# Moving one modulation vector, regrouping a feed-forward and rewriting the last norm of a two-layer diffusion transformer on one core

## The chip, the cores and the metric

The kernel runs on one core of a Trainium2 chip. The metric is device time in microseconds (us) of one execution. The kernel before takes 1594.34 us, the median of 3 runs (1590.8 to 1597.15). The profiled execution, from which all rows below come, took 1595.19 us.

## The reference

Two transformer layers over 512 latent tokens and 256 context tokens, width 1024, all float32. Layer 0 has eight neighbourhood-attention (NA) heads and eight latent-attention (MLA) heads side by side, one output projection and a SwiGLU feed-forward of width 2816. Layer 1 has 16 sliding-window heads and the same kind of feed-forward. The context tokens pass layer 0 too. Cut to what matters here:

```
def rms_norm(x, gain=None):
    y = x * rsqrt(mean(x * x, axis=-1) + EPS)          # optionally times gain
def modulate(x, shift, scale):
    return rms_norm(x) * (1 + scale) + shift
# per layer: six vectors from c (and from c_ctx for the context): shift, scale, gate of attention and of feed-forward
mods = silu(c) @ mod_w[l] + mod_b[l]
x = x + gate_a * (heads(modulate(x, shift_a, scale_a)) @ w_out)
h = modulate(x, shift_f, scale_f)
x = x + gate_f * (silu(h @ w_g) * (h @ w_u)) @ w_down
out = rms_norm(x_latent_after_layer_1, final_norm)
```

Inside the MLA heads the compressed queries and keys are normalised as well, with gains of their own.

## The kernel before, in words

Activations lie transposed: 128 features on the partitions, 768 tokens (512 latent, `LATS`, then 256 context, `CTXS`) along the row, 8 such tiles (KT) for the width. Every dense product keeps float32 precision by splitting both operands in a high and a low part and summing three matmuls, high·high, high·low, low·high; these are the lines L335, L337 and L338. A weight tile is loaded by the SyncE queue (SP) to a staging tile `wr`, cast by ScalarE (ACT) to `wh` and subtracted by VectorE (DVE) or GpSimd (POOL) to `wl`.

The program in order of time:

- up to about 60 us: loads, the first norm (`first_norm`, `norm_spread`), two modulation vectors (`mods_pe`) on TensorE (PE);
- to about 177 us: twelve projections of layer 0 (`projections`). After each of their 96 steps `bg` takes on average DBG = 0.38 steps of a background generator, `all_mods`, which computes the other modulation vectors;
- to about 265 us: the NA heads, two at a time (`na_jobs`). While a pair of heads runs, `step` draws on side jobs that `beside` has put in a list (ORDER, by pair; STEPS says how many heads' steps pass between draws): splitting later operands, `latent_norms`, which calls `gained`, and `mla_prepare`;
- to about 400 us: the MLA heads and the output projection;
- to about 1000 us: feed-forward 0. Its 22 hidden panels are worked off in groups (CHUNKS: first panel, count). After each group the down projection adds to a residual kept in DRAM (`home`). The last group goes through `final0`, which calls `output` with two streams, first the latent tokens, then the context, and collects sums of squares for the next norm (`norm1`) while it does so;
- to the end: layer 1, its feed-forward, and `final1`, which calls `output` with two halves of 256 latent tokens and writes the result.

Scale, shift and gate vectors of six are counted by `comp`: 0 shift, 1 scale, 2 gate of attention; 3, 4, 5 the same of the feed-forward. The scale of feed-forward 0, comp 4, belongs to the ones computed on TensorE: four chunks of eight 32-row matmuls (L209, weights in tiles `ph` and `pl` loaded by SP, 16 loads of 256 KB), a copy of the partial sums, and two selecting matmuls with `pick` (L213) that add the partial sums of the 32-row groups. Here they come from `all_mods`, in the middle of the projections.

A norm's reciprocal root is a column, one value per token, and is needed along the row. `rstd` (L388 to L397) sums squares with matmuls against `ones`, takes the root on ACT, the reciprocal on DVE (L391), multiplies the identity by the column (L392, "diag") and multiplies by `ones` on TensorE (L397), all in plain float32. `first_norm` with `norm_spread` (L802, L812) and `gained` (L988, L992) do the same.

The order on each engine is set by a scheduler that simulates the program while it is built (`schedule_with_timeline_sim`); `behind` and `in_turn` add orderings by hand. Every engine, and every DMA queue, then works in its fixed order. Tile tags are rings: `wr`, `wh` and `wl` have three buffers each, PSUM tags s, t, o and d have 3, 2, 1 and 2 banks.

Of the kernel before, what the change touches and what calls it, by code (L numbers as in the profile page):

```python
# [27 lines left out]
CHUNKS = ((0, 4), (4, 4), (8, 4), (12, 4), (16, 3), (19, 3)), ((0, 3), (3, 3), (6, 4), (10, 4), (14, 4), (18, 4))  # L28
# [26 lines left out]
ORDER = ("2", "n3", "m", "")  # L55
AFTER = "012k5678"
DBG = 0.38
# [14 lines left out]
STEPS = ((2, 3, 4, 4), 5, 3)  # L72
# [26 lines left out]
def hybrid_kernel(ctx: ExitStack, tc, I, out):  # L99
# [92 lines left out]
    def mods_pe(l, comp, get):  # L192
# [4 lines left out]
        for c in range(4):  # L197
            o = get()
            for k in range(KT):
                if k % 2 == 0:  # L200
# [9 lines left out]
            t, d = T("p", [P, NX]), get()  # L210
# [86 lines left out]
    def all_mods():  # L297
        for comp in (2, 4, 3, 5):
            yield from component(0, comp)
        for comp in (1, 0):  # L300
            yield from component(1, comp)
        for comp in (2, 4, 3, 5):
            for m in range(KT):
                yield from mod_tile(1, comp, m, (0,))
# [40 lines left out]
    def PQ():  # L345
        return PS("d")
# [32 lines left out]
    def rstd(acc, nfeat, c, r, get=PQ, tag="p"):  # L379
# [4 lines left out]
        col, diag = T("sm", [P, 6, 2]), B(tag=tag)  # L384
        col = col.rearrange("p a b -> p (a b)")[:, :m]
        for i in range(m):
            for j, a in enumerate(accs):
                marks["sum"] = PE.matmul(d[:, i : i + 1], a[:, i * P : (i + 1) * P], ones[:, :1], start=j == 0,  # L388
                                         stop=j == len(accs) - 1)
        marks["root"] = S.activation(col, d[:, :m], AF.Sqrt, bias=eps, scale=1.0 / nfeat)  # L390
        V.reciprocal(col, col)  # L391
        marks["diag"] = V.tensor_tensor(diag[:, :n].rearrange("p (a b) -> p a b", b=P), ident.unsqueeze(1).to_broadcast([P, m, P]),  # L392
                                        col.unsqueeze(2).to_broadcast([P, m, P]), op=ALU.mult)
        for i in range(0, n, 512):
            w = min(512, n - i)
            d = get() if r is not None else PS("o")
            marks["spread"] = PE.matmul(d[:, :w], ones, diag[:, i : i + w], start=True, stop=True)  # L397
# [28 lines left out]
    class Norm:  # L426
# [5 lines left out]
        def add(self, k, c):  # L432
            if c is self.two:
                self.acc = self.acc if k else [None, None]
                i = k // 4
                self.acc[i] = square_sum(self.acc[i], self.src[k], c, eng=(G, V)[i])
                if k == KT - 2:
                    n = c.stop - c.start
                    V.tensor_tensor(self.acc[1][:, :n], self.acc[1][:, :n], self.acc[0][:, :n], op=ALU.add)
                    self.acc[0] = None  # L440
# [358 lines left out]
    def first_norm(acc, c):  # L799
        n, d = (c.stop - c.start) // P, PM()  # L800
        col, diag = T("sm", [P, 6, 2]).rearrange("p a b -> p (a b)")[:, :n], B(tag="p")
# [928 lines left out]
```

## Time and profile before

| what | value |
| --- | --- |
| time, median of 3 | 1594.34 us (1590.8 to 1597.15) |
| profiled execution | 1595.19 us |
| its span, first to last instruction | 1593.4 us |
| mean granted clock of TensorE | 0.988 |
| busy: PE, DVE, ACT, POOL | 96%, 74%, 50%, 19% |
| data moved by DMA | 214.91 MB |

1.8 us of the profiled execution lie outside its span. A row of a timeline reads: start, duration, engine, line, operation, out<-in by the program's names, shape, count, and in brackets the idle time of the engine before it and what ended that. Matmuls are pipelined, so that their durations overlap; the distance from one start to the next is what one costs. A row of the windows reads: stretch, length, busy time of PE, of the weight loads (PEld), of DVE, ACT and POOL with counts, granted TensorE clock, busy share of the DMA engines, GB/s.

### The profile page before, as it was taken

How to read it: one execution, taken by the hardware profiler on the slowest of the kernel's cores; microseconds unless marked ns; L12 is line 12 of the kernel's file. 1: busy time of each engine (PE TensorE's matmuls, PEld its weight loads, DVE VectorE, ACT ScalarE, POOL GpSimd, SP SyncE). 2: the span in 40 equal slices, each digit the busy share in tenths (PEclk: the TensorE clock that was granted, in tenths of full speed). 3: DMA queues.
4: the chain of work that ended last, by engine and by line, in shares of the span. 5: the costliest groups of instructions: out<-in, count | busy, mean ns of one | idle time of the engine just before them, and what ended most of it. 6: DMA issues, size and time to landing. Idle time of an engine off the chain costs nothing. (4 is left out here: it accounts for less than half of the span.)

```text
span 1593.4 us, 26482 instructions
## 1 busy us (share of the span) xinstructions
PE 1533.9 (96%) x9966; PEld 1371.9 (86%) x9966; DVE 1177.1 (74%) x2348; ACT 797.9 (50%) x1615; POOL 299.3 (19%) x322
## 2 busy tenths in 40 slices
PE   6999999999999999999999998999999999999997
PEld 4787767787899999999989896877889899899997
DVE  4885877576678587796858686878877778678685
ACT  4563676775455243342424243557755545354453
POOL 0144623320011101102021202493012000000002
PEclk9999999999999999999999998999999999999998
DMA  9745332104343555637464756121015133324222
GB/s 309 252 129 178 84 117 59 23 6 159 129 162 127 190 168 167 215 114 289 152 248 158 268 165 248 61 87 60 2 46 168 47 100 126 107 79 133 87 93 80
DMA packets 76544, 214.91 MB, mean 135 GB/s; under 512 B 9952, under 2 KB 17504, under 8 KB 76416
## 3 DMA queue, kind: packets, MB, share of 16 engines
q1 hardware_dynamic: 57568, 141.79, 27.0%
q0 software_dynamic: 15968, 67.24, 12.2%
q10 hardware_dynamic: 2880, 4.20, 0.7%
q8 instruction: 78, 1.28, 0.3%
q14 instruction: 50, 0.41, 0.1%
HBM read 186.97 MB, written 23.07 MB: 132 GB/s over the span
## 5 line engine op out<-in xcount | busy, mean ns | idle before, releaser
L324 ACT CAST wh<-wr 128x1024 fp32r<-128x1024 f32 (+2 forms) x148 | 114.7, 789 | 199.8 <-DMA wr<-in_w_dn_dram 35.4
L325 DVE TENSOR_TENSOR wl<-wr,wh 128x1024 fp32r<-128x1024 f32 (+2 forms) x145 | 134.0, 930 | 81.6 <-ACT wh L324 79.9
L555 ACT ACTIVATE p<-p,sm 128x512 f32<-128x512 f32 (+3 forms) x144 | 105.0, 730 | 30.2 <-DVE sm L559 28.3
L376 POOL TENSOR_TENSOR p<-p,p 128x256 f32<-128x256 f32 (+1 forms) x33 | 32.2, 976 | 465.0 <-PE psd L338 340.5
L1372 PE MATMUL pss<-b,wh 128*128 128x384 f32 (+1 forms) x344 | 107.0, 311 | 0.6 <-ACT b L361 0.6
L1373 PE MATMUL pss<-b,wh 128*128 128x384 f32 (+1 forms) x344 | 107.2, 312 | 0.1
L1374 PE MATMUL pss<-b,wl 128*128 128x384 f32 (+1 forms) x344 | 106.2, 312 | 0.4 <-DVE wl L1360 0.4
L233 DVE CUSTOM_DVE_ANT_0 p<-rope,cond 128x1024 bf16<-128x1024 f32 x64 | 77.2, 1222 | 38.3 <-DMA rope<-in_mod_w_dram 38.3
L337 PE MATMUL psd<-b,wh 128*128 128x512 f32 (+3 forms) x256 | 87.9, 344 | 0.0
L335 PE MATMUL psd<-b,wh 128*128 128x512 f32 (+3 forms) x216 | 78.5, 364 | 0.5 <-ACT wh L324 0.3
L549 PE MATMUL pso<-ph,b 128*64 128x256 f32 (+1 forms) x384 | 77.5, 360 | 0.4 <-DVE ph L494 0.2
L549 PE MATMUL pso<-pl,b 128*64 128x256 f32 (+1 forms) x384 | 76.7, 359 | 0.7 <-DVE pl L494 0.7
L338 PE MATMUL psd<-b,wl 128*128 128x512 f32 (+3 forms) x216 | 76.6, 355 | 0.1
L228 POOL DMA_DIRECT2D rope<-in_mod_w_dram x48 | 25.5, 531 | 239.7 <-DVE mod L233 227.0
L1374 PE MATMUL pst<-b,wl 128*128 128x384 f32 (+1 forms) x224 | 70.1, 313 | 0.0
L1373 PE MATMUL pst<-b,wh 128*128 128x384 f32 (+1 forms) x224 | 69.9, 312 | 0.0
L1372 PE MATMUL pst<-b,wh 128*128 128x384 f32 (+1 forms) x224 | 69.9, 312 | 0.0
L335 PE MATMUL pss<-st,wh 128*128 128x512 f32 (+2 forms) x200 | 68.2, 342 | 1.6 <-ACT st L1173 0.8
L338 PE MATMUL pss<-st,wl 128*128 128x512 f32 (+2 forms) x200 | 68.0, 341 | 0.0
L337 PE MATMUL pss<-b,wh 128*128 128x256 f32 (+3 forms) x211 | 67.9, 322 | 0.1
L749 PE MATMUL pss<-st,st 128*128 128x256 f32 (+3 forms) x194 | 60.3, 333 | 6.2 <-DVE sm L559 5.9
L1372 PEld LDWEIGHTS pss<-b,wh 128*128 128x128 f32 x344 | 65.2, 190 | 1.1 <-ACT b L361 0.9
(666 smaller groups left out, 5412.9 us busy)
## 6 DMA issues: line engine op xcount, KB each, us to landing
wr<-in_w_gu_dram SPq DMA_DIRECT2D x88, 512.0 KB, 4.1
rope<-in_mod_w_dram POOLq DMA_DIRECT2D x48, 512.0 KB, 3.8
wr<-in_w_out_dram SPq DMA_DIRECT2D x32, 512.0 KB, 3.5
wr<-in_w_dn_dram SPq DMA_DIRECT2D x64, 256.0 KB, 3.0
p<-home POOLq DMA_DIRECT2D x40, 384.0 KB, 5.4
home<-p POOLq DMA_DIRECT2D x40, 384.0 KB, 4.9
wr<-in_w_in_dram SPq DMA_DIRECT2D x21, 512.0 KB, 4.1
nb<-in_nb_dram SPq DMA_DIRECT2D x16, 384.0 KB, 3.1
```

What stands on the lines that cost most here:

```text
L233: V.tensor_tensor_reduce(out=T("p", [P, D], mybir.dt.bfloat16), in0=w, in1=cond[:, v, :], op0=ALU.mult, op1=ALU.add, scale=1.0, scalar=0.0 ...
L324: behind(S.copy(h, r), *after[:1])
L325: behind((G if eng else V).tensor_tensor(lo, r, f(h), op=ALU.subtract), *after[1:])
L335: ins = PE.matmul(o, wh[:, k], mh[:, c], start=first and k == 0, stop=False)
L337: PE.matmul(o, wh[:, k], ml[:, c], start=False, stop=False)
L338: PE.matmul(o, wl[:, k], mh[:, c], start=False, stop=last and k == n - 1)
L549: ins = PE.matmul(o[64 * i : 64 * i + 64, c], v(kt), t, start=n == 0, stop=n == len(moving[i]) - 1)
L555: S.activation(p[:, c], p[:, c], AF.Exp, bias=nm, scale=-1.0, accum_out=dn)
L749: PE.matmul(o, x, ks[0][:, keys], start=True, stop=False)
L1372: PE.matmul(o, wh, xh, start=first and k == 0, stop=False, skip_group_check=not first)
L1373: PE.matmul(o, wh, xl, start=False, stop=False, skip_group_check=not first)
L1374: PE.matmul(o, wl, xh, start=False, stop=k == 3, skip_group_check=not first)
```

## The change

It has six parts.

1. Scale of feed-forward 0. comp 4 leaves `all_mods`. A new side job "s" (`scales`) runs it beside the first pair of NA heads. Its weights are now loaded by POOL's queue, as two 128x512 loads into each of a `wh` and a `wl` buffer per chunk, and the partial sums are copied to a `wr` buffer. DBG goes from 0.38 to 0.335 and the first entry of STEPS from (2, 3) to (6, 4).
2. Groups of feed-forward 0. The last two of (16, 3) and (19, 3) become (16, 4) and (20, 2). The down weights of the last group, now 2 panels, come by `keep_groups` in three loads (768, 768 and 512 columns) that are issued before the body of the last panel pair; before, eight loads of 384 columns came one for each output row (`kept_w`).
3. Spread of reciprocal roots. In `rstd`, `first_norm` with `norm_spread` and `gained` the diag multiply and the float32 matmul with `ones` go; `spread`, a TensorE transpose of the column broadcast to 128x128, comes in, one for each 128 tokens. In `gained` (by the new `gain`) DVE reads the spread values from PSUM; the ACT copies to SBUF go.
4. `Norm.add` keeps four partial sums (rows 0 to 3, 4 and 5, 6, 7) instead of two that are added at the end; the summing matmuls become 16 for the 512 latent tokens.
5. Parking the residual of layer 1 in DRAM: eight stores move from the ACT queue to the SP queue.
6. `final1` is written out: its own four partial sums per half, the square-root table of ACT asked for right after the last silu, the outputs of the first half two at a time between the matmuls of the second half's rows 5 to 7 and after them, their stores all on SP, the last eight outputs alternating between SP and ACT as before.

```
-CHUNKS = (... (12, 4), (16, 3), (19, 3)), ...
+CHUNKS = (... (12, 4), (16, 4), (20, 2)), ...
-ORDER = ("2", "n3", "m", "")
-DBG = 0.38
-STEPS = ((2, 3, 4, 4), 5, 3)
+ORDER = ("2s", "n3", "m", "")
+DBG = 0.335
+STEPS = ((6, 4, 4, 4), 5, 3)
...
-    def mods_pe(l, comp, get):
+    def mods_pe(l, comp, get, wide=None):
...
+                if k % 4 == 0 and wide:
+                    ws = T(wide[k // 4], [P, 1024])
+                    for i in range(2):
+                        G.dma_start(ws[:, 512 * i : 512 * i + 512], I["mod_wp"][PE_MODS.index((l, comp)), c, k // 2 + i])
...
-            t, d = T("p", [P, NX]), get()
+            t, d = T("wr" if wide else "p", [P, NX]), get()
...
-        for comp in (2, 4, 3, 5):
+        for comp in (2, 3, 5):
             yield from component(0, comp)
...
+    def scales():
+        yield from mods_pe(0, 4, PQ, ("wh", "wl"))
...
-        V.reciprocal(col, col)
-        marks["diag"] = V.tensor_tensor(diag[:, :n].rearrange("p (a b) -> p a b", b=P), ident.unsqueeze(1).to_broadcast([P, m, P]),
-                                        col.unsqueeze(2).to_broadcast([P, m, P]), op=ALU.mult)
+        marks["diag"] = V.reciprocal(col, col)
...
-            marks["spread"] = PE.matmul(d[:, :w], ones, diag[:, i : i + w], start=True, stop=True)
+            for j in range(0, w, P):
+                at = (i + j) // P
+                marks["spread"] = spread(d[:, j : j + P], col[:, at : at + 1].to_broadcast([P, P]))
...
+    def gain(tiles, g0, col):
+        for c in (LATS, CTXS):
+            d, n = PQ(), c.stop - c.start
+            for i in range(n // P):
+                at = c.start // P + i
+                spread(d[:, i * P : (i + 1) * P], col[:, at : at + 1].to_broadcast([P, P]))
+            for j, t in enumerate(tiles):
+                V.scalar_tensor_tensor(t[:, c], t[:, c], gains[:, g0 + j : g0 + j + 1], d[:, :n], op0=ALU.mult, op1=ALU.mult)
+        return tiles
...
+    def keep_groups(k0, kc):
+        n = NT // (kc * P)
+        for a in range(0, KT, n):
+            z = min(a + n, KT)
+            r, t = T("wr", [P, n * kc * P]), [T("nb", [P, NT], F32R) if a == 0 else B(F32R, "st") for _ in range(2)]
...
+                    if l == 0 and j == NFF - 1:
+                        keep_groups(k0, kc)
                     p.body()
...
-        behind(S.dma_start(t, H[k][:, LATS]), norm1.marks[0]["root"])
+        behind(nc.sync.dma_start(t, H[k][:, LATS]), norm1.marks[0]["root"])
...
     def final1(src, hs):
-        keep = lambda src, m: ahead.get(m) or load_w(src(m), len(hs), P, None, "b")
-        output(src, hs, 1, 5, STREAMS1, Norm(H, finished, G if EF else None), (0, 0), None, keep, wait=1)
+        behind(S.activation(T("part", [P, 1]), eps, AF.Sqrt), marks["silu"])
...
+        for c in HALVES:
+            sq, turn = [], []
+            for m in range(KT):
...
+                elif m == 2:
+                    last, col, ins = root(first, PQ())
+                elif m == 3:
+                    d, last = factors(col)
+                elif m > 4:
+                    turn += outputs(d, HALVES[0], (2 * m - 10, 2 * m - 9), (nc.sync,))
...
+                turn.append(add_residual(m, o, 1, 5, 0, c))
+                turn += square(m, c, sq)
...
+        in_turn(turn[-1], ins, *outputs(d, c, range(KT), (nc.sync, S)))
```

In the changed kernel the lines from the scale chunks on lie 6 to 50 further down: L215 and L219 are L209 and L213 of before, L751 and L752 the score matmuls L749 and L750, L1372 the casts L1359.

PE, in the middle of the projections (`pss_1194` is the accumulator of a projection, `ph` and `pl` hold the scale's weights), before:

```order
L338 MATMUL pss_1194<-b_100,wl_1157 128x256
L209 MATMUL psd_1203<-ph_1204,cond_col_63 32x256 x2
L209 MATMUL psd_1203<-pl_1208,cond_col_63 32x256 x2
L209 MATMUL psd_1203<-ph_1212,cond_col_63 32x256 x2
L209 MATMUL psd_1203<-pl_1216,cond_col_63 32x256 x2
L335 MATMUL pss_1194<-b_102,wh_1156 128x256
```

PE, among the score matmuls of the first pair of NA heads, now:

```order
L752 MATMUL pss_1962<-st_657,st_653 128x256
L215 MATMUL psd_1819<-wh_1820,cond_col_63 32x256 x2
L751 MATMUL pss_1983<-st_656,st_653 128x512
L752 MATMUL pss_1983<-st_657,st_653 128x512
L215 MATMUL psd_1819<-wh_1820,cond_col_63 32x256 x2
L215 MATMUL psd_1819<-wl_1827,cond_col_63 32x256 x4
L219 MATMUL psd_1835<-pick_64,wr_1834 128x2 x2
L215 MATMUL psd_1841<-wh_1842,cond_col_63 32x256 x4
```

The chunks have left the rows of dense matmuls and stand in front of score matmuls. Their loads stand on POOL between the last background products (L278), the copies of values for the NA heads (L1139) and the splitting of their keys (L718), now:

```order
L278 TENSOR_TENSOR pl_1686<-pl_1686,cond_66 128x512
L718 TENSOR_TENSOR b_1746<-p_1389,b_1746 64x768
L203 DMA wh_1820<-in_mod_wp_dram 128x512 x2
L203 DMA wl_1827<-in_mod_wp_dram 128x512 x2
L203 DMA wh_1842<-in_mod_wp_dram 128x512 x2
L203 DMA wl_1849<-in_mod_wp_dram 128x512 x2
L718 TENSOR_TENSOR st_2117<-p_1549,st_2117 64x768
```

The third and fourth chunk's loads can only be issued once POOL has finished the L718 above them.

ACT, at the boundary from the last panel pair of feed-forward 0 to `final0` (casts `st<-wr` are those of the last group's down weights, casts `b<-p` and `st<-p` those of hidden panels, `wh` casts belong to the first weights of layer 1), before:

```order
L1359 CAST st_9877<-wr_9876 128x384
L1359 CAST st_9901<-wr_9900 128x384
L324 CAST wh_9896<-wr_9894 128x1024
L1427 ACTIVATE p_9617<-pst_9619 128x384
L1359 CAST st_9920<-wr_9919 128x384
L1359 CAST st_9940<-wr_9939 128x384
L1359 CAST b_9583<-p_9617 128x384 x2
L373 ACTIVATE p_9805<-b_9770 128x512
```

and now:

```order
L1372 CAST st_9728<-wr_9727 128x768
L1372 CAST st_9507<-p_9541 128x384
L1372 CAST st_9734<-wr_9733 128x512
L330 CAST wh_9899<-wr_9897 128x1024
L1435 COPY p_9659<-pss_9660 128x384
L330 CAST wh_9915<-wr_9913 128x1024
L1440 ACTIVATE p_9658<-pss_9660 128x384
L1372 CAST st_9624<-p_9658 128x384 x2
L379 ACTIVATE p_9856<-b_9824 128x512
```

No cast of a down weight stands between the last panel's activation (L1427, now L1440) and its own casts any more.

DVE, at the end (`b_…<-ps…` is the last residual, `p<-b,final_norm,pso` an output), before:

```order
L1223 SCALAR_TENSOR_TENSOR b_12147<-pss_16881,mod_1881_9427,b_12147 128x256
L1612 SCALAR_TENSOR_TENSOR p_16878<-b_12141,final_norm_12838,pso_16779 128x256
L1612 SCALAR_TENSOR_TENSOR p_16898<-b_12143,final_norm_12838,pso_16779 128x256
L1612 SCALAR_TENSOR_TENSOR p_16901<-b_12145,final_norm_12838,pso_16779 128x256
L1612 SCALAR_TENSOR_TENSOR p_16904<-b_12147,final_norm_12838,pso_16779 128x256
L376 TENSOR_TENSOR p_16752<-p_16752,p_16895 128x256
L391 RECIPROCAL sm_16908<-sm_16908 128x2
L392 TENSOR_TENSOR p_16909<-ident_r_86,sm_16908 128x256
```

and now:

```order
L1227 SCALAR_TENSOR_TENSOR b_12127<-pss_16864,mod_1817_9172,b_12127 128x256
L1658 SCALAR_TENSOR_TENSOR p_16880<-b_12125,final_norm_12816,pso_16777 128x256
L1658 SCALAR_TENSOR_TENSOR p_16883<-b_12127,final_norm_12816,pso_16777 128x256
L1648 RECIPROCAL sm_16895<-sm_16895 128x2
L1658 SCALAR_TENSOR_TENSOR p_16901<-b_12113,final_norm_12816,pso_16898 128x256
```

Behind the last residual two outputs of the first half are left instead of four, and the sum (L376) and the diag (L392) are gone.

121 lines of the change are left out of this document (75 added, 46 removed).

## The prediction

> **What bounds the kernel now.** I read the page's engine table and its slices first, then the table of waits, then windows of the stages that the change touches, and last PE's rows at the edges of each.
>
> ```profile
> span 1593.4 us, 26482 instructions
> PE 1533.9 (96%) x9966; PEld 1371.9 (86%) x9966; DVE 1177.1 (74%) x2348; ACT 797.9 (50%) x1615; POOL 299.3 (19%) x322
> PE   6999999999999999999999998999999999999997
> PEclk9999999999999999999999998999999999999998
> ```
>
> PE is busy for 96% of the span, and lacks work in three places: the first slice, the 25th (956 to 996 us) and the last. The granted clock falls in the last two as well. An edit gains by taking time from PE's own row, or by closing those three places; DVE, ACT and POOL matter only where PE waits for them.
>
> ```profile
> 120.00:140.00 20.00, 20.00 (x137) 13.26 (x136) 6.01 (x17) 5.60 (x12) 2.98 (x2) 1.00 0.81 289
> 180.00:200.00 20.00, 17.74 (x140) 14.41 (x140) 16.77 (x45) 16.51 (x44) 13.00 (x8) 1.00 0.47 129
> 200.00:240.00 40.00, 36.14 (x243) 27.75 (x244) 28.76 (x67) 31.41 (x72) 10.78 (x9) 0.91 0.35 113
> 960.00:1000.00 40.00, 33.02 (x168) 27.95 (x168) 25.48 (x43) 15.12 (x28) 12.09 (x16) 0.87 0.67 248
> 1560.00:1594.00 34.00, 22.84 (x177) 21.77 (x176) 18.81 (x44) 9.94 (x22) 8.91 (x12) 0.84 0.20 68
> ```
>
> These windows price the stages. In the projections (120 to 140) PE has no gap: whatever leaves this row is won in full. Beside the first neighbourhood heads PE is idle for 2.3 of 20 us, then for 3.9 of 40: work put there is partly free. The boundary at 960 to 1000 leaves PE idle for 7.0 us at a clock of 0.87, and the last 34 us leave 11.2.
>
> **The change part by part.** *Scale chunks leaving the projections.* On PE each of the four chunks lies between a last L338 of a dense row and the next L335:
>
> ```profile
> 116.80 0.28 PE L338 MATMUL pss<-b,wl 128*128 128x256 f32 x1
> 118.01 0.39 PE L335 MATMUL pss<-b,wh 128*128 128x256 f32 x1
> ...
> 120.14 0.28 PE L338 MATMUL pss<-b,wl 128*128 128x256 f32 x1
> 122.03 0.50 PE L335 MATMUL psd<-b,wh 128*128 128x512 f32 x1
> ...
> 124.66 0.39 PE L338 MATMUL psd<-b,wl 128*128 128x512 f32 x1
> 127.63 0.50 PE L335 MATMUL psd<-b,wh 128*128 128x512 f32 x1
> ...
> 131.44 0.28 PE L338 MATMUL psd<-b,wl 128*128 128x256 f32 x1
> 131.56 0.50 PE L213 MATMUL pss<-pick,p 128*128 128x2 f32 x4
> 132.99 0.39 PE L335 MATMUL psd<-b,wh 128*128 128x256 f32 x1
> ```
>
> A 256-wide dense matmul costs 0.12 (131.44 to the next start at 131.56), a 512-wide one twice that, so the pieces cost 118.01 − 116.80 − 0.12 = 1.09, then 1.77, 2.73 and 1.43: 7.0 us, all of it saved there. The same matmuls come back beside the heads, about 1.0 for the eight of a chunk (the first gap holds just these) and 0.5 for the selecting ones, 6 us in all. The floor of what is paid is 0 (idle time of 2.3 + 3.9 = 6.2 us up to 240 us covers them), the ceiling without a stall 7.0. That idle time is waits for softmax, which do not vanish for being filled:
>
> ```profile
> PE pss L749 <- DVE sm L559: 7.7, 9, 1.8
> ```
>
> Nine waits of 0.9 us each: a chunk of 1.5 us fills one and overhangs by 0.6, and only if the scheduler put it at one. I take half, 3.5 paid, so −3.5 net (−7 to 0). The ACT copies and DVE adds move with the chunks; both engines had the same ones before, and DVE has 3.2 of 20 us free in the window at 180.
>
> What could stop PE is the loads. They change queue, from SP to POOL:
>
> ```profile
> ph<-in_mod_wp_dram SPq DMA_DIRECT2D x16, 256.0 KB, 5.1
> rope<-in_mod_wp_dram POOLq DMA_DIRECT2D x8, 256.0 KB, 3.9
> ```
>
> A load of this size from POOL's queue lands 3.9 us after issue, no slower than from SP. But POOL works in order, and the last two chunks' loads stand behind its own work, of which the longest piece near is
>
> ```profile
> 179.53 2.41 POOL L716 TENSOR_TENSOR b<-p,b 64x768 fp32r<-64x768 f32 x1
> ```
>
> In the trace POOL ends its second L716 at about 185 us, when PE is at the same score matmuls behind which the third chunk now stands; both move about 7 us earlier together. PE may wait up to a landing there, and I leave this inside the 3.5.
>
> *Spread of the latent norms (`gained`).* A float32 matmul against `ones` makes way for transposes:
>
> ```profile
> L992 PE MATMUL psd<-b,ones 128*128 128x512 f32 x4 | 3.2, 886 | 1.2 <-DVE b L988 1.2
> 262.15 0.66 PE L503 MATMUL psd<-ident_r,p 128*128 128x128 f32 x4 [0.19 <-ACT b L468]
> ```
>
> The four L992 entries carry 3.2 us of PE and 1.2 of waiting; each row holds the 512-wide and the 256-wide pair of one group. Four transposes take 0.66, so the twelve take 2.0. PE saves 3.2 + 1.2 − 2.0 = 2.4 at most, nothing if its neighbours then wait for the same DVE results; DVE also loses a diag for each group, so I take −2 (−2.4 to 0).
>
> *Boundary of feed-forward 0.* The number of groups stays six, so residual traffic and the sum of matmuls are unchanged. What changes is what the last panel pair waits for:
>
> ```profile
> 972.13 0.58 PE L335 MATMUL psd<-st,st 128*128 128x512 f32 x1 [2.49 <-DVE p L1429]
> 976.77 0.80 PE L335 MATMUL pst<-b,nb 128*128 128x512 f32 x1 [1.94 <-ACT b L1359]
> 990.19 1.05 PE L388 MATMUL pss<-ones,p 128*128 128x1 f32 x8 [2.56 <-DVE p L376]
> ...
> 974.06 0.51 ACT L1359 CAST st<-wr 128x384 fp32r<-128x384 f32 x1 [3.94 <-DMA wr<-in_w_dn_dram]
> ...
> 970.00:975.00 5.00, 2.71 (x6) 1.62 (x6) 2.38 (x6) 1.05 (x3) 0.38 (x1) 0.73 1.02 402
> 975.00:980.00 5.00, 3.23 (x8) 2.56 (x9) 1.74 (x5) 0.51 (x1) 0.00 (x0) 0.50 1.02 404
> ```
>
> ACT waits 3.94 us for a down-weight load (974.06) before it may cast the hidden panel that stands behind it, and DMA is saturated, share 1.02, while the clock halves. The new order has no such cast there and takes the down weights earlier, in three loads. The three waits are worth 2.5 + 1.9 + 2.6 = 7.0. The clock adds the missing part of it, (1 − 0.73) × 2.71 + (1 − 0.50) × 3.23 = 2.3 us of PE's busy time in those ten. So 9.3 at most from these ten microseconds and the norm; four partial sums shorten the 2.56 in front of the norm's sums (one add of DVE less, against 8 more small matmuls: 1.05 for 8, so +1.0). Against it, the context stream, under which that norm hides, loses a panel: 8 rows × 3 matmuls × 0.12 = 2.9 us of cover. I take −7 (−11 to −2): the first two waits and the clock nearly in full (6.7), the norm's wait by a little.
>
> *End.* The last rows before:
>
> ```profile
> 1580.33 0.28 PE L338 MATMUL pss<-st,b 128*128 128x256 f32 x1
> 1581.80 1.70 DVE L1612 SCALAR_TENSOR_TENSOR p<-b,final_norm,pso 128x256 f32<-128x256 f32 x4 [0.29 <-DMA out_dram<-p]
> 1583.42 0.42 DVE L376 TENSOR_TENSOR p<-p,p 128x256 f32<-128x256 f32 x1
> 1583.89 1.01 PE L388 MATMUL psd<-ones,p 128*128 128x1 f32 x4 [3.28 <-DVE p L376]
> 1585.43 0.42 DVE L392 TENSOR_TENSOR p<-ident_r,sm 128x256 f32<-128x256 f32 x1
> 1585.91 1.22 PE L397 MATMUL pso<-p,ones 128*128 128x256 f32 x2 [1.01 <-DVE p L392]
> 1587.17 3.22 DVE L1612 SCALAR_TENSOR_TENSOR p<-b,final_norm,pso 128x256 f32<-128x256 f32 x8 [1.31 <-PE pso L397]
> ```
>
> Between the last product and the sums lie four outputs of the first half (1.70) and an add (0.42) on DVE; both leave that chain, as the sum of row 7 needs its square alone. The diag (0.42) goes, and the spread falls from 1.22 to two transposes, 0.3 by the row above: −0.9. The sums grow from 4 to 8 matmuls, of which six can run before the last square: taken as 0. Together 1.70 + 0.42 + 0.42 + 0.9: −3.4. The eight outputs (3.22) and the stores stay. Bounds: −5 if the table request and the earlier first half also close part of the other gaps of the last 34 us, −2 if the two outputs still behind the last residual come in front of the reciprocal and cost 0.8 each way.
>
> *Start and the remaining norms.*
>
> ```profile
> PE pst L802 <- DVE p L376: 12.6, 1, 12.6
> 16.28 2.08 PE L812 MATMUL pst<-p,ones 128*128 128x512 f32 x2
> ```
>
> The first wait is for loads and squares, which stay. L812's 2.08 becomes six transposes, 1.0, with the diag in front gone, but the first projections wait for weights too: −1 (−1.5 to 0). The parking stores go from ACT to SP, where DMA issues cost PE nothing: 0; if SP holds a weight load of layer 1 behind them, eight of about 4 us would be visible as PE waits, which the other gaps there do not suggest.
>
> Sum: −3.5 − 2 − 7 − 3.4 − 1 = −16.9. The profiled execution took 1595.19, so 1578.3; the median is 0.85 below the profiled one. I forecast **1578**.
>
> **A page that speaks against it.** The Trainium skill, "TensorE: Matmul & The Clock Gate", section "Part 4: PE-mode transpose", says that transposes do not count as busy time for the clock. The trace speaks against a price here: the clock was 1.00 in a stage full of them.
>
> ```profile
> 280.00:320.00 40.00, 40.00 (x313) 32.50 (x310) 23.88 (x74) 28.58 (x66) 13.11 (x9) 1.00 0.09 20
> ```
>
> **The rivals.** *Loads stop the heads (slower).* If each chunk's loads are issued only after the POOL work in front of them and PE reaches the chunk when that work begins, PE waits 2.4 (L716) + 3.9 (landing) = 6.3 us a chunk, 25.2 for four, and the heads absorb nothing. Then 1595.2 − 7.0 + 7.0 + 25.2 − 13.4 = 1607. It is slower than before from 13.4 / 4 = 3.4 us per chunk; with two chunks, 12.6, it is 1594, no change. For it: the loads stand behind L718 in POOL's order. Against it: only two chunks do, and POOL's idle time lies before them. The Trainium skill, "SBUF — State Buffer", section "SBUF: two separate sides", adds a way to it: a load issued from GpSimd waits for its descriptors while VectorE runs certain operations; the 3.9 us of POOL's loads against 5.1 of SP's do not show it. Chance 0.04.
>
> *The heads absorb nothing and the boundary half.* Scale 0, boundary −3.5, the others −1, −2 and −0.5: −7.0, 1588. For it: DMA was saturated at the boundary, and the same bytes still have to come; earlier loads may only shift the full stretch under the pair before. Chance 0.17.
>
> *The shorter context stream turns the norm into a wait.* The first layer-1 products need `norm1`; with 2.9 us less cover its chain, 1.05 of sums growing to 2.1, ends 4 us later against PE: boundary −3, total −13, 1582. Chance 0.17.
>
> *Transposes cool the clock.* If the clock fell to one half for the norm's 2 to 5 us at four places, some 2 us each go: −9, 1586. Chance 0.05.
>
> *More than the sum.* All upper bounds of scale, boundary and end: −7 − 2 − 11 − 5 − 1 = −26, 1569. For it: the clock at the boundary stays full for longer than the ten microseconds counted, and 11.2 us idle lie in the last window. Chance 0.16.
>
> *Nothing happens:* the scheduler's new order elsewhere in the heads eats the gain, 1594. Chance 0.05.
>
> **How the numbers follow.** The forecast has 0.36, with its own range 1574 to 1582. The cases of 1588 and 1569 belong in the range with their own spread of 2, and I let it end at 1567 and 1590; 1594, 1605 and the tails stay outside, about 0.15. A measurement of this kernel can tell about 0.5%, 8 us, from no change: faster than 1586.4 are the forecast, the norm's wait, the big gain and about half of the 0.22 that lies at 1586 to 1588, 0.80; within it the rest of these and the case of nothing, 0.16; slower 0.04.
>
> **What would show it.** Between 115 and 135 us L338 is followed by L335 without a gap, and the projections end 7 us earlier. Between 170 and 200 PE shows no wait of more than 2 us for a load into `wh` or `wl`; four of 5 us or more would make the slower rival true. At the boundary no ACT cast waits for `w_dn`, the three PE gaps of 1.9 to 2.6 shrink below 1, and the clock stays over 0.9; a new wait of 3 us or more in front of the sums or of layer 1's first products would be the norm's rival. From the last product to the last instruction it is 9.5 us instead of 13. If the projections end earlier but the neighbourhood heads end at the old time, the term of the scale chunks was wrong.

## The result, and the profile after

The changed kernel takes 1605.26 us, the median of 5 runs (1601.7 to 1607.25); the kernel before took 1594.34 (1590.8 to 1597.51). The ratio is 1.0061, with a 95% interval of 1.0041 to 1.0081: slower by 0.4 to 0.8%, where 1578 was forecast. The page of the profiled execution, in the rows that were shown of before:

```profile
span 1605.4 us, 26540 instructions
PE 1543.9 (96%) x10024; PEld 1383.4 (86%) x10024; DVE 1168.4 (73%) x2331; ACT 797.2 (50%) x1607; POOL 303.9 (19%) x332
PE   6999889999999999999999999999999999999998
PEclk9999789999999999999999999999999999999999
```

The gap in the 25th slice is closed, as forecast, and the last slice is a little fuller (8 tenths busy instead of 7). Instead, PE is less busy and its clock falls in slices 5 and 6 (161 to 241 us), where the neighbourhood heads run. The windows:

```profile
100.00:110.00 10.00, 8.21 (x38) 6.65 (x37) 9.78 (x21) 5.73 (x15) 7.42 (x5) 0.83 0.40 116
180.00:200.00 20.00, 14.14 (x77) 8.58 (x77) 11.11 (x25) 10.29 (x25) 15.26 (x14) 0.61 0.74 224
200.00:240.00 40.00, 32.68 (x229) 26.53 (x230) 25.74 (x59) 24.63 (x57) 8.99 (x7) 0.88 0.25 73
960.00:1000.00 40.00, 38.26 (x203) 34.76 (x202) 30.54 (x50) 17.41 (x31) 8.00 (x12) 1.00 0.78 275
1000.00:1005.00 5.00, 5.00 (x38) 4.85 (x38) 2.03 (x3) 1.78 (x2) 0.70 (x1) 0.85 0.34 129
1005.00:1010.00 5.00, 5.00 (x25) 5.00 (x25) 2.00 (x5) 1.71 (x5) 2.19 (x3) 0.50 0.17 39
1560.00:1606.00 46.00, 38.32 (x321) 37.93 (x319) 25.59 (x56) 17.25 (x38) 4.59 (x6) 0.94 0.25 75
```

From 180 to 200 us PE is idle for 5.9 us instead of 2.3 and runs at a clock of 0.61; up to 240 another 7.3 us are idle, where it was 3.9.

To see where time was lost and won I put both timelines of PE side by side and took the time at which the same product stands: the first score matmul of the neighbourhood heads, the first of the MLA heads, the first pair product of feed-forward 0, its 1135th (inside the fourth group), the first product of layer 1, the last pair product of feed-forward 1, and the end of the span. Each number is that time minus the time in the profile of before; what a stage costs is the difference of two neighbours.

| profile of | heads | MLA | FF0 | FF0, group 4 | layer 1 | FF1 last | span |
| --- | --- | --- | --- | --- | --- | --- | --- |
| the change | -3.4 | +10.5 | +9.3 | +16.5 | +12.2 | +14.3 | +12.0 |
| e1, without part 1 | -0.4 | -9.2 | -10.3 | -7.2 | -6.6 | -4.3 | -5.7 |
| e2, part 1 alone | -3.3 | +10.6 | +10.6 | +12.7 | +9.9 | +14.2 | +14.2 |
| e3, quarter loads | -3.8 | -2.0 | -1.8 | +6.1 | +0.8 | +2.5 | +0.5 |
| e4, loads on SP | -5.5 | -2.9 | -7.0 | -4.0 | -7.3 | -5.0 | -7.3 |
| e12, last two on SP | -3.6 | -3.1 | -7.2 | -4.8 | -7.9 | -6.6 | -9.0 |
| e5, part 3 alone | -1.8 | -12.1 | -13.6 | -10.9 | -11.0 | -9.6 | -11.6 |
| e13, part 3 with copies | -1.4 | -11.3 | -12.9 | -10.2 | -12.7 | -11.4 | -13.1 |
| e6, part 2 alone | +1.3 | -3.8 | -4.1 | -3.9 | -5.2 | -1.9 | -2.1 |
| e7, part 6 alone | +2.1 | +0.2 | -0.3 | -1.0 | -0.3 | +0.2 | -1.6 |
| e8, without parts 1 and 2 | -1.7 | -7.7 | -8.6 | -6.6 | -4.8 | -4.5 | -6.7 |
| e9, part 4 alone | -0.7 | -3.6 | -3.8 | -3.5 | -3.5 | -3.2 | -3.6 |
| e11, e4 with DBG 0.295 | -4.7 | -3.2 | -1.0 | +1.3 | -2.1 | -0.8 | -2.6 |

By this table the change won 3.4 us up to the heads, lost 13.9 in the heads, won 1.2 up to feed-forward 0, lost 7.2 in its groups, won 4.3 at the boundary to layer 1, lost 2.1 in layer 1 and won 2.3 at the end: 12.0 us lost. One profile is one execution, and how much that matters can be read from e6, e7 and e9: up to 398 us their four compute engines run the same instructions in the same order as before, and yet their heads take 5.1, 1.9 and 2.9 us less than in the profile of before. So differences of less than about 5 us in the heads mean little, and 13.9 does. For the time of a kernel the medians count: the profile of e1 lies 4.8 us above its own median, that of e5 4.5 below.

What stands in the heads: POOL's rows, then PE's waits of over 1 us (the first row is from the projections).

```profile
179.97 1.82 POOL L718 TENSOR_TENSOR b<-p,b 64x768 fp32r<-64x768 f32 x1
181.73 1.12 POOL L203 DMA_DIRECT2D wh<-in_mod_wp_dram  x2
182.84 1.06 POOL L203 DMA_DIRECT2D wl<-in_mod_wp_dram  x2
183.90 1.06 POOL L203 DMA_DIRECT2D wh<-in_mod_wp_dram  x2
184.95 1.07 POOL L203 DMA_DIRECT2D wl<-in_mod_wp_dram  x2
```

```profile
104.44 0.50 PE L344 MATMUL pss<-b,wl 128*128 128x512 f32 x1 [1.79 <-DVE wl L331]
...
183.90 0.47 PE L751 MATMUL pss<-st,st 128*128 128x512 f32 x1 [1.66 <-DVE sm L561]
195.87 0.58 PE L751 MATMUL pss<-st,st 128*128 128x256 f32 x1 [3.23 <-DVE sm L561]
229.07 0.69 PE L551 MATMUL pso<-pl,b 128*64 128x256 f32 x1 [2.19 <-ACT pl L497]
239.14 0.53 PE L751 MATMUL pss<-b,b 128*128 128x192 f32 x1 [2.87 <-DVE sm L561]
```

The loads of the third and fourth chunk, 2 MB, leave POOL between 181.7 and 186.0, straight behind the second L718. In the same microseconds the heads need a bias tile (`nb`), which SP asks for at 185.65. It usually lands 3.1 us after its issue; in this profile one took 9.3, and DVE stood for it:

```profile
DMA to landing us min/median/max: 2.9/3.1/9.3
```

```profile
195.11 0.69 DVE L561 CUSTOM_DVE_ANT_0 p<-pss,nb 128x512 f32<-128x512 f32 x1 [2.13 <-DMA nb<-in_nb_dram]
```

Before, the slowest landing of a bias tile in these 80 us was 3.3 us by the same view. The scale loads land late in the same burst: their view (L203) has a median of 4.3 us and a longest landing of 9.2. PE's list of waits from 176 to 262 us shows for whom it waited, longest first:

```profile
PE pss L751 <- DVE sm L561: 8.6, 4, 3.2
PE pso L551 <- ACT pl L497: 2.2, 1, 2.2
PE psd L219 <- ACT wr L217: 1.4, 3, 0.5
```

No row of that list is a load into `wh` or `wl`. PE stands for the softmax sums on DVE, and these stand once for a bias tile, once behind PE's own chunks: in PE's order the third chunk lies in pieces around a score matmul that DVE waits for.

```profile
186.07 1.07 PE L215 MATMUL psd<-wh,cond_col 128*32 128x256 f32 x4
187.07 0.80 PE L751 MATMUL pss<-st,st 128*128 128x512 f32 x1
188.22 0.64 PE L215 MATMUL psd<-wh,cond_col 128*32 128x256 f32 x2
191.55 1.08 PE L215 MATMUL psd<-wh,cond_col 128*32 128x256 f32 x8
```

### The profile page after: what moved, and what is told of

Read it like the earlier page. It is cut to its first block, busy times and chain, and to the rows that moved or that the text cites. A ratio compares the mean times of both kernels' runs of the same rounds, so it can differ in the third digit from the quotient of the medians.

```text
span 1605.4 us, 26540 instructions
## 1 busy us (share of the span) xinstructions
PE 1543.9 (96%) x10024; PEld 1383.4 (86%) x10024; DVE 1168.4 (73%) x2331; ACT 797.2 (50%) x1607; POOL 303.9 (19%) x332
## 3 DMA queue, kind: packets, MB, share of 16 engines
q0 software_dynamic: 17248, 71.43, 12.9%
## 5 line engine op out<-in xcount | busy, mean ns | idle before, releaser
L330 ACT CAST wh<-wr 128x1024 fp32r<-128x1024 f32 (+2 forms) x148 | 115.5, 795 | 210.8 <-PE pss L343 38.3
L343 PE MATMUL psd<-b,wh 128*128 128x256 f32 (+2 forms) x258 | 86.8, 337 | 2.0 <-DVE b L1373 1.8
L1387 PE MATMUL pss<-b,wl 128*128 128x256 f32 (+1 forms) x258 | 79.7, 309 | 2.3 <-DVE wl L1373 2.2
L551 PE MATMUL pso<-pl,b 128*64 128x256 f32 (+1 forms) x384 | 78.9, 365 | 2.9 <-ACT pl L497 2.2
L343 PE MATMUL pss<-b,wh 128*128 128x256 f32 (+3 forms) x242 | 79.8, 331 | 0.0
L1385 PE MATMUL pss<-b,wh 128*128 128x256 f32 (+1 forms) x258 | 79.5, 308 | 0.0
L1386 PE MATMUL pss<-b,wh 128*128 128x256 f32 (+1 forms) x258 | 79.3, 307 | 0.0
L551 PE MATMUL pso<-ph,b 128*64 128x256 f32 (+1 forms) x384 | 79.0, 364 | 0.3 <-DVE ph L496 0.2
L341 PE MATMUL pss<-st,wh 128*128 128x256 f32 (+2 forms) x231 | 78.5, 340 | 0.4 <-ACT wh L330 0.4
L344 PE MATMUL pss<-st,wl 128*128 128x512 f32 (+2 forms) x231 | 78.0, 338 | 0.0
L341 PE MATMUL psd<-b,wh 128*128 128x512 f32 (+2 forms) x218 | 76.6, 351 | 0.7 <-DVE st L738 0.7
L344 PE MATMUL psd<-b,wl 128*128 128x512 f32 (+2 forms) x218 | 75.6, 347 | 0.7 <-DVE wl L331 0.6
L1385 PE MATMUL pst<-b,wh 128*128 128x384 f32 (+1 forms) x234 | 72.3, 309 | 0.5 <-ACT b L367 0.5
L1386 PE MATMUL pst<-b,wh 128*128 128x384 f32 (+1 forms) x234 | 72.3, 309 | 0.0
L751 PE MATMUL pss<-st,st 128*128 128x256 f32 (+3 forms) x194 | 61.5, 339 | 7.8 <-DVE sm L561 7.7
L1387 PE MATMUL psd<-b,wl 128*128 128x384 f32 (+1 forms) x210 | 65.2, 313 | 2.7 <-DVE wl L1373 2.7
```

Source lines behind the costliest of these rows:

```text
L330: behind(S.copy(h, r), *after[:1])
L341: ins = PE.matmul(o, wh[:, k], mh[:, c], start=first and k == 0, stop=False)
L343: PE.matmul(o, wh[:, k], ml[:, c], start=False, stop=False)
L344: PE.matmul(o, wl[:, k], mh[:, c], start=False, stop=last and k == n - 1)
L551: ins = PE.matmul(o[64 * i : 64 * i + 64, c], v(kt), t, start=n == 0, stop=n == len(moving[i]) - 1)
L751: PE.matmul(o, x, ks[0][:, keys], start=True, stop=False)
```

## The experiments

All are edits of one of the two kernels; "part" counts as in the list of the change. Each was timed in rounds beside the kernel before; the ratio is to that, and its median in the same group of runs is given where the group changes. The scheduler builds every edit anew, so that an edit can move instructions that it does not name; where the traces show that, the text says so.

**e1: part 1 undone.**

```
-ORDER = ("2s", "n3", "m", "")
+ORDER = ("2", "n3", "m", "")
-DBG = 0.335
+DBG = 0.38
-STEPS = ((6, 4, 4, 4), 5, 3)
+STEPS = ((2, 3, 4, 4), 5, 3)
-        for comp in (2, 3, 5):
+        for comp in (2, 4, 3, 5):
```

> The changed kernel with part 1 undone: the scale chunks go back into the projections, the five other parts stay. Theory A (the scale loads fill the DMA engines while the heads wait for their bias tiles, the stall halves the clock, and this outweighs the rest): the projections end about 3 us later than in the changed kernel, the heads come out 10 to 14 us earlier, and the time is 1590 to 1596. Theory B (the loads are late only because they stand behind POOL's work): the same, 1590 to 1596. Theory C (the scheduler's new order, not the loads, costs the time all over the kernel): no more than 4 us of change, 1601 or more.

Measured 1584.66 us against 1595.19 of before, ratio 0.9950 (0.9935 to 0.9965). With the other five parts in place, moving the scale chunks costs 20.6 us (1605.26 against 1584.66), more than A and B expected, and turns a gain into a loss. Theory C falls. The heads come out 19.7 us earlier than in the change (-9.2 against +10.5).

**e2: the kernel before with part 1 alone.**

```
+ORDER, DBG, STEPS, all_mods, mods_pe and scales as in the change; nothing else
```

> The kernel before with part 1 alone. Theories A and B: slower than before by 8 to 14 us, 1602 to 1608, with the loss between 183 and 240 us. Theory C: within 4 us of before.

1610.97 us, ratio 1.0112 (1.0089 to 1.0135), in A's and B's direction and a little beyond. The heads lose 13.9 us, as in the change. Theory C falls here too.

**e3: a quarter of the bytes.** Each load brings 128 of 512 columns and all matmuls of a chunk use them; the scale of feed-forward 0 is then not the reference's.

```
-                    ws = T(wide[k // 4], [P, 1024])
+                    ws = T(wide[k // 4], [P, 512])
-                        G.dma_start(ws[:, 512 * i : 512 * i + 512], I["mod_wp"][..., c, k // 2 + i])
+                        G.dma_start(ws[:, 128 * i : 128 * i + 128], I["mod_wp"][..., c, k // 2][:, 128 * i : 128 * i + 128])
```

> The changed kernel with a quarter of the bytes in the scale loads: each chunk's two loads per buffer bring 128 columns instead of 512, and all eight matmuls use these (so the scale of feed-forward 0 is not the reference's). Number of loads, queue, order and matmuls stay. Theory A: the bias loads land in about 3 us again, PE's wait near 190 us goes, and the time falls by 6 to 12 us, to 1593 to 1599. Theory B: the loads are as late as before, so no more than 3 us. Theory C: no more than 4 us.

1595.49 us, ratio 1.0003 (0.9984 to 1.0022): 10 us won, as A expected. The loads stand at the same place behind POOL's work. They land in 2.2 us, bias tiles in 4.0 at most, and the heads lose 1.8 us instead of 13.9. From 176 to about 208 us the order on POOL and DVE is that of the change, and that on PE and ACT too, but for four chunk matmuls and one copy; there the bytes alone bring the first product with the values (L551) from 204.3 to 200.2 us. Behind that the order differs, so that the larger half of the gain in the heads is not the bytes' alone.

```profile
wh<-in_mod_wp_dram POOLq DMA_DIRECT2D x8, 64.0 KB, 2.2
wl<-in_mod_wp_dram POOLq DMA_DIRECT2D x8, 64.0 KB, 2.2
```

**e4: all scale loads on SP.**

```
-                        G.dma_start(ws[:, 512 * i : 512 * i + 512], ...
+                        nc.sync.dma_start(ws[:, 512 * i : 512 * i + 512], ...
```

> The changed kernel with the scale loads issued by SP instead of POOL. Theory B: the third and fourth chunk's loads no longer wait behind POOL's work, the stall near 190 us goes, 1593 to 1598. Theory A: the same bytes still meet the bias loads, on whose queue they now stand, so 1601 to 1609. Theory C: within 4 us of the changed kernel.

1587.19 us, ratio 0.9948 (0.9933 to 0.9964): 18 us won with the same bytes, in B's direction and beyond its 1593 to 1598; A did not expect it. Bytes alone are not the cause. PE's order is another one here, though: all of the third and fourth chunk stands in front of the 512-wide score matmul that it lay around in the change.

**e12: only the third and fourth chunk's loads on SP.** The edit names nothing but the queue. The expectation takes PE's order around the chunks to be that of the change; the trace shows that it is not.

```
+                        (G if c < 2 else nc.sync).dma_start(ws[:, 512 * i : 512 * i + 512], ...
```

> The changed kernel with only the third and fourth chunk's loads on SP; the first two stay on POOL. PE's order around them is that of the changed kernel. Theory B (the loads behind POOL's L718 are late and arrive in one burst on top of the bias load): these two carry the loss, so 1586 to 1591. Rival (any load on POOL's queue costs the heads, by POOL's issue time or otherwise): half of the gain of moving all four, 1594 to 1599.

1587.22 us against 1593.17, ratio 0.9964 (0.9945 to 0.9983), inside B's range: the loss against the kernel before hangs on the queue of these two chunks' loads. SP's and PE's timelines, and the windows to be set beside those of the change:

```profile
179.62 0.81 SPq L203 DMA_DIRECT2D wh<-in_mod_wp_dram  x2
180.59 0.80 SPq L203 DMA_DIRECT2D wl<-in_mod_wp_dram  x2
```

```profile
181.91 0.64 PE L215 MATMUL psd<-wh,cond_col 128*32 128x256 f32 x8
184.46 0.64 PE L215 MATMUL psd<-wh,cond_col 128*32 128x256 f32 x8
187.89 0.50 PE L751 MATMUL pss<-st,st 128*128 128x512 f32 x1 [1.94 <-DVE sm L561]
```

```profile
180.00:200.00 20.00, 16.25 (x143) 13.22 (x142) 12.93 (x39) 14.20 (x37) 10.04 (x6) 1.00 0.56 178
200.00:240.00 40.00, 36.58 (x281) 28.16 (x280) 32.48 (x75) 31.16 (x74) 11.98 (x9) 1.00 0.38 118
```

The last loads leave at 181.4 instead of 186.0, the chunks run at 181.9 and 184.5 instead of 186 to 197, and the clock is 1.00 in these windows. With the queue the order has changed on PE, DVE and ACT: the chunks now fill the place where PE stood idle in the change (182.2 to 183.9), in front of the score matmul instead of around it, and DVE's splitting of keys (L732, 4.75 us in one piece in the change) comes behind the softmax. A first reading of mine, that the bias tile is the price, is too simple: in e12 DVE waits 6.1 us in all for bias tiles, in the change 6.5, and yet PE keeps its clock. A and B each hold part of it: loads behind POOL's L718 leave late (B) and come in one burst with the bias load (A); less of the burst (e3) or another queue (e4, e12) takes away most of the loss. No run moves the loads with the order of the engines held, so that lateness and the order that the scheduler makes of it are not told apart.

**e5: the kernel before with part 3 alone**, the spreads by transposes in `rstd`, `first_norm`, `norm_spread` and `gained`, as in the diff of the change.

> The kernel before with part 3 alone (the spreads by transposes in the start, the norms and the latent norms). The scale-less run left the neighbourhood heads 8.8 us earlier against before, though this part was priced at -2 there. Theory A (the spread through DVE and float32 matmuls stalled PE and with it cost clock near 210 and 245 us, so that its removal is worth several times its own duration): the heads end 6 to 9 us earlier and the time is 1585 to 1590. Theory B (the 8.8 us come from another part's effect on the order): 1590 to 1594, the heads 0 to 3 us earlier.

1588.10 us against 1592.18, ratio 0.9959 (0.9942 to 0.9975): 4 us won. In its profile the heads win 10.3 us, more than A's 6 to 9, but against the heads of e6, e7 and e9, which are those of before, it is 5.2 to 8.4. Two windows of e5 answer the two cold places of before:

```profile
210.00:220.00 10.00, 9.65 (x73) 7.83 (x72) 8.82 (x21) 9.21 (x23) 5.21 (x6) 1.00 0.24 68
240.00:250.00 10.00, 9.83 (x78) 8.23 (x77) 8.46 (x18) 7.46 (x18) 1.41 (x2) 1.00 0.32 92
```

The same windows of the kernel before:

```profile
210.00:220.00 10.00, 8.70 (x35) 5.57 (x34) 5.25 (x13) 6.72 (x16) 2.35 (x1) 0.66 0.22 68
240.00:250.00 10.00, 7.38 (x47) 6.72 (x43) 7.31 (x12) 3.23 (x11) 4.64 (x4) 0.76 0.00 1
```

Only the first of the two belongs to the program: from 208 to 220 us e6, e7 and e9 have clocks of 0.72 to 0.78 as before has (0.72), but from 240 to 250 all three have 1.00.

**e13: e5 with the copies of the spread values to SBUF kept**, so that only the diag and the float32 matmuls go.

```
+            S.copy(r[:, c], d[:, :n])
+        for j, t in enumerate(tiles):
+            V.scalar_tensor_tensor(t, t, gains[:, g0 + j : g0 + j + 1], r, op0=ALU.mult, op1=ALU.mult)
```

> The kernel before with part 3 alone (1588.1), but with ACT's copies of the spread values to SBUF kept in the latent norms, so that only the diag on DVE and the float32 matmuls go. Theory A (the float32 matmul chain behind the diag held PE and cooled its clock): the heads keep the gain, MLA begins at 250 to 255 us, 1586 to 1590. Theory B (ACT's and DVE's time for the copies held the softmax): the gain goes, MLA begins at 259 us or later, 1590 to 1594.

1585.31 us against 1593.17, ratio 0.9951 (0.9931 to 0.9971), MLA begins at 252.9, A's case with a time just below its range. The copies cost nothing here. What is left is the chain of diag and float32 matmuls; which of the two, and how much the order that changes with them, no run tells.

**e6: the kernel before with part 2 alone**, CHUNKS, `keep_groups` and the two places in `ffn` that call it.

> The kernel before with part 2 alone (groups of 4 and 2, down weights of the last group in three loads). By the prediction the boundary gains 7 us: 1585 to 1590. Rival (the waits at the boundary move into the new four-panel group, and the shorter context stream shows the norm): 1592 to 1597.

1592.86 us against 1592.18, ratio 1.0010 (0.9996 to 1.0024): the time is the rival's. At the boundary the two waits of before are gone and another has come, in front of the sums of the norm:

```profile
984.96 1.87 PE L388 MATMUL pss<-ones,p 128*128 128x1 f32 x8 [4.48 <-DVE p L376]
```

**e7: the kernel before with part 6 alone**, `final1` as in the change.

> The kernel before with part 6 alone (the written-out end). By the prediction -3.4: 1590 to 1592.5, from the last product to the end 9.5 us instead of 13. Rival (the outputs and sums among the second half's products cost PE what the end saves): 1593.5 to 1596, the last dense product 3 us later.

1592.07 us against 1592.18, ratio 0.9997 (0.9979 to 1.0014), no change that can be told; the time lies in the expected range only because the kernel before was as fast in this group. In the profile the span is 1.6 us shorter: the end wins, and the second half's products give some of it back.

**e8: the change without parts 1 and 2.**

> The changed kernel with parts 1 and 2 undone. If the groups bring their 7 us, this is 5 to 8 us slower than the kernel with part 1 alone undone (1584.7): 1589 to 1593. If they bring nothing or cost, it is at most 1586.

1587.98 us against 1592.18, ratio 0.9968 (0.9954 to 0.9982), between the two expectations. With part 2 (e1) it was 0.9950; the intervals overlap, and 2 to 3 us for the groups with four partial sums is all that can be read from it, not 7.

**e9: the kernel before with part 4 alone.**

```
-                i = k // 4
-                self.acc[i] = square_sum(self.acc[i], self.src[k], c, eng=(G, V)[i])
-                if k == KT - 2: ...
+                i = (k > 3) + (k > 5) + (k > 6)
+                self.acc[i] = square_sum(self.acc[i], self.src[k], c, eng=(G, V)[min(i, 1)])
```

> The kernel before with part 4 alone (four partial sums in the norm of the latent tokens of layer 1, so 16 summing matmuls of one column instead of 4). By the prediction this is worth 0 to -1: 1593 to 1594. Theory A (the one-column matmuls cost 4.5 us instead of 1 and cool the clock, as the changed kernel's rows at 1000 to 1010 us show): the wait in front of the sums goes but the window behind them has a clock near one half, so no gain from the boundary: 1594 to 1598.

1593.95 us against 1594.21, ratio 1.0000 (0.9982 to 1.0017), as the prediction had it, just outside A. Its sums take the time that the wait took:

```profile
984.08 3.40 PE L388 MATMUL pss<-ones,p 128*128 128x1 f32 x30
```

**e10: e4 with two partial sums** (rows 0 to 6, and 7).

```
-                i = (k > 3) + (k > 5) + (k > 6)
+                i = (k > 3) + (k > 6)
+                if k == KT - 2: ... acc[1] += acc[0] on DVE, acc[0] = None
```

> The changed kernel with the scale loads on SP (1587.2) and two partial sums instead of four in that norm (rows 0 to 6 joined by one add, row 7 alone: 8 summing matmuls). Theory A of the sums: 2 to 5 us faster than with four, 1582 to 1585. Rival (the add makes the sums wait as in the run of the groups alone, 4.5 us): 1587 to 1590.

1588.97 us, ratio 0.9963 (0.9950 to 0.9976): nothing won against e4 (0.9948), and the rival's wait is there with 2.7 us.

```profile
981.87 2.34 PE L393 MATMUL pst<-ones,p 128*128 128x1 f32 x16 [2.66 <-DVE p L445]
```

**e11: e4 with fewer background steps in the projections** (DBG 0.335 to 0.295).

> The changed kernel with the scale loads on SP (1587.2) and DBG at 0.295 instead of 0.335, so 28 background steps instead of 32 in the projections. Of the 7 us that the chunks' leaving should bring in the projections only 3 came. Theory A (DVE works off more background products per projection and makes PE wait for a low weight part near 104 us, which also halves the clock): the wait goes, the heads start 2 to 4 us earlier, 1583 to 1586. Rival (the work left over stalls a later stage): 1587 or more.

1591.71 us, ratio 0.9988 (0.9976 to 1.0000). A miss for A, as the rival had it: the wait near 104 us is unchanged. Between the MLA heads and feed-forward 0, where the work left over is caught up, the profile loses 2.2 us against before, while e4 wins 4.1.

```profile
104.20 0.50 PE L344 MATMUL pss<-b,wl 128*128 128x512 f32 x1 [1.79 <-DVE wl L331]
```

The fastest kernels beat both: e4, e1 and e13 with 0.9948 to 0.9951, which these runs do not tell apart.

## Why the prediction was wrong

The step that failed is the second half of the first part: the scale chunks beside the heads, priced at 3.5 us with 0 to 7 as bounds. Part 1 was to win 3.5 us as a whole and costs 20.6 (e1 against the change); that is 24 of the 27 us by which the forecast of 1578 missed. In the heads the change loses 13.9 us where e1, which differs by part 1, wins 8.8: 22.7 for the chunks. Two things make up this price.

The larger one is the sentence "PE may wait up to a landing there, and I leave this inside the 3.5". The queue of the last two chunks' loads, with the order that comes of it, is worth 13.4 us in the heads: the change loses 13.9 there, e12 0.5. The rival of late loads came out near the measured time, 1607 against 1605, but by luck. It has PE wait 6.3 us for the loads of each of four chunks; PE's list shows no wait for such a load, only two chunks were late, and for two the rival itself gives 1594. What it had right is the place, and that POOL's order was on record: the text itself says that the loads stand behind L718, and gave it a chance of 0.04. A part of the 13.4 was no landing at all: the first product with the values comes at 204.3 in the change and at 194.9 in e12, so that some 4 us of it arose later.

The smaller one needs no late load. With the loads on SP the heads still lose 0.5 to 2.6 us (e12, e4), where without part 1 they win 6.0 to 8.8 (e8, e1): 6.5 to 11.4 us for the chunks instead of 3.5. The "nine waits of 0.9 us" that they were to fill are those of the whole kernel; the same view for 165 to 265 us has five, 4.3 us in all.

The clock shows in the price, but does not set it alone. In the change PE's idle time of 1.7 us at 182 and of 3.2 at 193 goes with a clock of one half from 184 to 204, as this window shows:

```profile
184.00:204.00 20.00, 15.80 (x76) 10.45 (x76) 10.47 (x23) 9.79 (x23) 11.26 (x9) 0.51 0.63 193
```

15.8 us busy at one half are some 8 us of work. But e4 stands at 0.50 from 188 to 192 and e3 from 192 to 200, and they lose 2.6 and 1.8 us. Nor does the length of a gap tell whether the clock falls: e2 has a gap of 1.6 us at the place of the change's 1.7, and in the 4 us behind it the clock is 0.53 in the change and 1.00 in e2:

```profile
184.00:188.00 4.00, 4.00 (x14) 2.22 (x14) 1.10 (x5) 3.95 (x8) 3.86 (x6) 0.53 0.84 270
184.00:188.00 4.00, 3.67 (x24) 1.77 (x25) 1.28 (x5) 3.95 (x8) 3.94 (x6) 1.00 0.88 305
```

The Trainium skill, "TensorE: Matmul & The Clock Gate", section "Part 1: The HAM clock gate (the "warmup" mystery)", says that the clock follows activity in a window that runs freely and is not reset when a kernel starts. These runs agree with that but cannot show the window itself. The second stall, 229 to 239 us, also goes in e4 and e12. In the change the casts of the query weights, whose loads SP issued at 225.2 and 229.9 and before at 214.7 and 222.0, stand before softmax work on ACT; that they are the link is argued, no run isolates it.

*Leaving the projections, -7.0.* It was -3.0 (from -0.4 at the first dense product to -3.4). The row at 104.44 shows a wait of 1.8 for a low weight part and the window at 100 to 110 a clock of 0.83, both absent in e1, which has the chunks back. That DVE's other background products stand closer without comp 4's steps is argued; that fewer steps cure it was wrong (e11), so this is open.

*Latent norms, -2 (-2.4 to 0).* Part 3, forecast at 3 us with its share in the start, wins 4.1 alone by the medians (e5) and 7.9 with the copies kept (e13); the heads win 5.2 to 10.3 us in e5, by the profile that one compares with. The step left out the clock: it is 0.66 in the window at 210, where the float32 matmuls stand behind a wait of 1.8 for the softmax and 1.2 for the diag, and 1.00 in e5. Whether the matmuls or the waits cool it is not shown. With the late loads nothing of this gain is left: part 1 alone (e2) and the whole change both lose 13.9 in the heads. Two terms that live in the same idle places of 60 us are not a sum. What the prediction quoted from the Trainium skill, "TensorE: Matmul & The Clock Gate", section "Part 4: PE-mode transpose", was turned into a rival; transposes did not cool the clock in e5, and the rival did not come.

*Boundary, -7 (-11 to -2).* It was -4.3 in the profile; by the medians part 2 brings nothing alone (e6) and 2 to 3 us at most with the rest (e8). The waits at 972 and 977 went, and the window 960 to 1000 is busy for 38.3 of 40 at a clock of 1.00, which was the step as forecast. What failed is the price of the sums, "+1.0" for more small matmuls:

```profile
1000.75 4.55 PE L393 MATMUL pst<-ones,p 128*128 128x1 f32 x32
1009.15 1.05 PE L373 MATMUL pso<-ident_r,sm 128*128 128x128 f32 x4
```

4.55 us stand where 1.05 stood; the prediction took the 8 entries of before for eight matmuls, but they are four, so that twelve more cost 3.5. PE counts as busy there, and the clock falls to 0.50 right behind. With e6's wait of 4.5 and e9's and e10's rows the rival of the norm was right in kind: short sums make it wait, long ones take the time themselves.

*End, -3.4.* Right by its own chain, but not in the time:

```profile
1595.79 0.28 PE L344 MATMUL pss<-st,b 128*128 128x256 f32 x1
1597.62 0.61 PE L1643 MATMUL psd<-ones,p 128*128 128x1 f32 x4 [0.31 <-ACT p L1664]
1598.87 0.41 PE L373 MATMUL pso<-ident_r,sm 128*128 128x128 f32 x2 [0.65 <-DVE sm L1648]
1599.31 3.22 DVE L1658 SCALAR_TENSOR_TENSOR p<-b,final_norm,pso 128x256 f32<-128x256 f32 x8 [0.59 <-PE pso L373]
```

From the last product to the last outputs it is 3.5 us instead of 6.8, 3.3 won. But from the last pair product to the last dense one it grew from 20.9 to 22.0: the first half's sums and spread stand among those products. Net -2.3 in the profile; alone the part changes nothing that can be told (e7).

Together the five parts without part 1 win 10.5 us (e1) of the 13.4 that were forecast for them. That this comes so near is in part luck: part 3 brought more than its term, the boundary and the end less.

*Feed-forward 0 up to its fourth group* had no term, and 7.2 us went there in the change, 7.9 in e3. PE waits there for DVE's `wl` (2.7 us at 806; e4 1.3, e12 0.9). e4 and e12, whose PE order there is the same, lose 2.4 to 3.0. What sets it is open; the program of the stage does not differ between these runs.

*Parking stores on SP* were not tested alone.

## What to carry to other kernels

A load that moves to another queue is priced by what stands ahead of it on that queue at that time, chunk by chunk, from the new order's rows; if two of four stand behind compute work and their reader is on the bounding engine, that is the forecast and not a rival. Where a scheduler builds the order, such a move also moves the readers, so that an experiment on the queue has to be set beside both orders. Gaps in one stage are not a budget to be spent twice: a part that fills them and a part that closes them cannot both be counted. Before a difference between two profiles is given a cause, executions of one and the same program show how much it takes: here 5 us in the heads.

## What the runs showed of the hardware

One-column matmuls keep PE busy for 4.55 us by the profile and the clock drops to 0.50 behind them (1005 to 1010 us). In e9, with the same 16 sums, the two 5 us windows from 985 to 995 are at 0.81 and 0.85. Behind the four sums of before (990 to 995) it is 1.00.

With 2 MB of loads issued in 4.3 us from POOL, a bias tile of 384 KB issued among them from SP landed in 9.3 us instead of 3.1.
